# The first two jobs of the first output projection, placed ahead of the last two projection jobs of the first layer

## The chip, the cores and the metric

The kernel runs on one core of one Trainium2 chip. The metric is device time in microseconds, as the median of the runs of a kernel; lower is better. Engines are named as in the profile: PE (TensorE matmul), PEld (its weight loads), DVE (VectorE), ACT (ScalarE), POOL (GpSimd) and SP (SyncE, which issues the DMAs here).

## What is computed

Two layers on a sequence of 2048 frames with 1024 features, each `x = x + gate * Mixer(RMSNorm(x) * (1 + scale) + shift)`, and a final RMSNorm. The change lies at the end of the first layer, whose mixer is a gated linear recurrence:

```python
def rglru_block(h, in_w, conv_w, conv_b, gate_w, gate_b, lam, out_w):
    proj = h @ in_w
    xb, zg = proj[..., :D_RNN], proj[..., D_RNN:]
    xb = causal_dwconv(xb, conv_w) + conv_b
    pre = einsum('bsni,knij->kbsnj', xb.reshape(...), gate_w) + gate_b
    r_t, i_t = sigmoid(pre)
    log_a = -RG_C * r_t * softplus(-lam)
    a_t = exp(log_a)
    b_t = sqrt(-expm1(2.0 * log_a)) * (i_t * xb)
    _, hseq = lax.associative_scan(_lin_combine, (a_t, b_t), axis=1)
    return (hseq * silu(zg)) @ out_w
```

The second layer's mixer is a chunked gated delta rule with its own input and output projections; its first input weights are already being loaded while the first layer ends.

## The kernel before

**Tiles.** All matrix products are made of 128x512 results. Each factor is split into a high and a low part, and a product of depth 1024 takes 8 depth tiles of three matmuls each: high by high, low by high, high by low. One such product, 24 matmuls into one PSUM bank, is a **job** (`job` L663 for input projections, `out1_jobs` L933 for the first output projection; both call `products`, whose matmul is L668). PSUM has four bank pairs, called `mm`, `d`, `c` and `tp`.

**The end of the first layer.** The sequence is handled in two units of 1024 frames, each in two halves of 512. Of the second unit the last four input jobs are, in order: x panel 7 on half 0, z panel 7 on half 0, x panel 7 on half 1, z panel 7 on half 1 (named x70, z70, x71 and z71 below; in the trace the tiles `hh_('in1', 1)_1833` belong to half 0, `..._2277` to half 1). An x job's result goes through the convolution (ACT `xf` L746, `edge` L752, three DVE taps L756), is split into `xh` (ACT L798) and `xl` (DVE L801), and then PE makes two gate products `pg` of three matmuls each (L807). Behind these come ACT tanh `tg` (L857), `th`, `tg` (L817, L819), a square root (L830, with a table load ahead of it), DVE steps, a scan (L838), and POOL's product with `tz` (L845), which SP stores as `y_d` (L849). A z job's result goes through ACT tanh `tz` (L783) and DVE (L785).

**The first output projection.** Its 32 jobs take, for two blocks of 128 frames at a time, column half d=0 of both blocks and then column half d=1 of both. Its left factor `yh`, `yl` (ACT L925, DVE L929) comes from `y_d`. d=0 uses the bank pair `mm` and d=1 the pair `d`. A job's result waits for a tile `xr` of the input (SP L970), is multiplied with the gate and added to `xr` on DVE (L954, L956), and stored to `x1_d` (SP L959). The `xr` tiles share two places with `xl`, and their loads begin only when x71's `xl` has its place.

**Weights, and the two places they go through.** A weight panel is loaded by SP into `raw` (L606), cast on ACT to `whi` (L644), and POOL makes `wlo` from `raw` and `whi` (L650). There are two places for `raw`, two for `whi` and two for `wlo`. The output weights use the same two `raw` places: each column half is loaded in four parts `oraw` (SP L896), each split into `oh` (ACT L907) and `ol` (DVE L909). The weights of d=0 (`oh_2402`) are ready long before. Those of d=1 (`oh_3984`) take the room of z70's input, so their splits begin after z70. The `raw` places are taken, in this order, by: the second layer's first panel, d=1 part 0, the second layer's second panel, and d=1 parts 1, 2 and 3. The second layer's first `whi` takes the place of x panel 7, so its cast waits for x71's last matmul.

**The order of the work.** Every step is a generator, and `Weave` lays them out before the kernel runs: it picks the thread that can start first by a table of assumed durations, then by priority. The result is a fixed list of instructions for each engine and for SP, which each engine works through in order. `project_thread` (L698) is the thread that runs all projection jobs one after another.

Of the kernel before, what the change touches and what calls it, by code (L numbers as in the profile page):

```python
# [19 lines left out]
NU = S // T  # L20
# [119 lines left out]
def trunk_kernel(ctx, tc, x, c, ada_w, ada_b, ada_c, norm_c, final_g, w1, cw1, cb1, gate_w, gate_b, lam, ow1,  # L140
# [91 lines left out]
    def ev(*key):  # L232
        return events.setdefault(key, Event())

    def put(tag, token):
        w.put(slots[tag], token)
# [344 lines left out]
    def pair(a, b):  # L581
        return [(p, i) for i in range(NTC) for p in (a, b)]

    plans = []
    for u in range(NU):
        panels = [(1, kind, n) for n in range(KT) for kind in "xz"]
        jobs = pair(*panels[:2]) + [(p, i) for p in panels[2:-2] for i in range(NTC)] + pair(*panels[-2:])
        plans.append((("in1", u), panels, jobs))
    plans.append((("out1",), [], []))
    for u in range(NU):  # L590
# [4 lines left out]
        jobs = pair(*panels[:2]) + [(p, i) for p in panels[2:-2] for i in range(NTC)] + pair(*panels[-2:])  # L595
# [65 lines left out]
    def products(pt, lhs, rhs, wait=None, dur=MM):  # L661

        for k in range(KT):  # L663
            if wait is not None:
                yield wait(k)
            for n, (a, b) in enumerate(((0, 0), (0, 1), (1, 0))):
                yield "pe", dur, 0.0
                pe.matmul(pt, lhsT=lhs[a][:, k, :], rhs=rhs[b][:, k, :], start=(k == 0 and n == 0),  # L668
                          stop=(k == KT - 1 and n == 2))

    def job(name, jobs, n):
        u = name[1]
        p, i = jobs[n]
        layer, kind, m = p
        hi, lo, htok, ltok = yield ev("w", name, p)
        h = yield ev("tiles", (name, i))
        rtok = None
        if layer == 2 and kind in "kq":
            rtok = yield slots[kind + "t"]

        bank = ("d" if layer == 1 else "c") if kind in "vz" else "mm"
        mtok = yield slots[bank]
        pt = ps.tile([P, TC], F32, tag=bank, name="mm")
        yield from products(pt, (hi, lo), h, (lambda k: ev("split", (name, i), k)), 0.2275 if layer == 1 else MM)
        if all(q != p for q, _ in jobs[n + 1:]):
            put("whi", htok)
            put("wlo", ltok)
        if layer == 1:
            w.spawn((conv1_thread if kind == "x" else z1_thread)(u, m, i, pt, mtok, bank), 2, 0.2)
        elif kind == "z":  # L690
            w.spawn(zgate_thread(u, m, i, pt, mtok, bank), 6, 0.2)
        else:
            w.spawn(conv2_thread(u, kind, m, i, pt, mtok, bank, rtok), 5, 0.2)
        if all(j != i for _, j in jobs[n + 1:]):
            w.set(ev("free", name, i))
        w.set(ev("job", name, n))

    def project_thread():  # L698
        for name, panels, jobs in plans:
            if name == ("out1",):  # L700
                yield from out1_jobs()
                continue
            for n in range(len(jobs)):
                if name == ("in1", 0) and n < 2:

                    w.spawn(job(name, jobs, n), 8 + n)
                    if n == 1:
                        yield ev("job", name, 0)
                        yield ev("job", name, 1)
                else:  # L710
                    yield from job(name, jobs, n)
        yield from out2_jobs()
# [217 lines left out]
            put("yf", tok)  # L930
            w.set(ev("yhl", b), (yh, yl, htok, ltok))

    def out1_jobs():  # L933
        nb = S // P
        jobs = [(b + q, d) for b in range(0, nb, 2) for d in range(2) for q in range(2)]
        for b, d in jobs:
            yh, yl, htok, ltok = yield ev("yhl", b)
            ow = yield ev("owtiles", 1, d)
            bank = "d" if d else "mm"
            mtok = yield slots[bank]  # L940
            pt = ps.tile([P, TC], F32, tag=bank, name="mmo")
            yield from products(pt, (yh, yl), ow, (lambda k: ev("ow", 1, d, k // 2 * 2)))
            if d == 1:
                put("yh", htok)
                put("yl", ltok)
            w.spawn(residual1_thread(b, d, pt, bank, mtok), 3, 0.2)
            if b == nb - 1:
                w.set(ev("free", "out1", d))

    def residual1_thread(b, d, pt, bank, mtok):  # L950
        xr, xtok = yield ev("xr", b, d)
        row = yield ev("gate", 0, d)
        yield "dve", EV
        dve.tensor_tensor(pt, pt, row[:, d * TC:(d + 1) * TC], ALU.mult)  # L954
        yield "dve", EV
        dve.tensor_tensor(xr, pt, xr, ALU.add)  # L956
        put(bank, mtok)
        yield "sp", 256 * KB
        sp.dma_start(out=x1_d[b * P:(b + 1) * P, d * TC:(d + 1) * TC], in_=xr)  # L959
        put("xr", xtok)  # L960
        w.set(ev("x1", b, d))
# [632 lines left out]
    def out2_jobs():  # L1594
        nb = S // P

        parts = {b: [(0, TC), (TC, TC)] for b in range(nb - 1)} | {nb - 1: [(0, TC), (TC, TC // 2), (TC + TC // 2, TC // 2)]}
        jobs = [(0, 0), (1, 0), (0, 1), (1, 1)] + [(b, q) for b in range(2, nb) for q in range(len(parts[b]))]
        for b, q in jobs:
            c0, n = parts[b][q]  # L1600
            d, o = divmod(c0, TC)
            yh, yl, htok, ltok = yield ev("ohl", b)
            ow = yield ev("owtiles", 2, d)
            if q == 0:
                w.spawn(finish_thread(b, len(parts[b])), 3, 3.0)
            mtok = yield slots["mm"]
            pt = ps.tile([P, n], F32, tag="mm", name="mmo")
            yield from products(pt, (yh, yl), [t[:, :, o:o + n] for t in ow],
                                (lambda k: ev("ow", 2, d, k // 2 * 2)), MM * n / TC)
            if q == len(parts[b]) - 1:  # L1610
                put(*htok)
                put(*ltok)
            w.spawn(final_thread(b, q, c0, n, pt, mtok), 3, 0.2)
# [63 lines left out]
    with tc.manual_schedule():  # L1677
# [3 lines left out]
        in1, in2 = [("in1", u) for u in range(NU)], [("in2", u) for u in range(NU)]  # L1681
# [7 lines left out]
        w.spawn(columns_thread(), 4)  # L1689
        w.spawn(panels_thread(), 1)  # L1690
        w.spawn(project_thread(), 9)
        w.spawn(lru_thread(), 4)
        w.spawn(row_halves_thread([(0, 2, 0), (0, 2, 1), (1, 0, 0), (1, 0, 1), (1, 1, 0), (1, 1, 1), (1, 2, 0),
# [95 lines left out]
```

## Time and profile before

| | us |
|---|---|
| runs | 1933.47, 1934.21, 1941.75 |
| median | 1934.21 |
| span of the profiled execution, first to last instruction | 1937.1 |
| PE busy in it | 1844.0 |
| DVE, ACT and POOL busy in it | 1471.2, 1048.2, 654.8 |

The profiled execution has no other time of its own than its span, which lies 2.9 us above the median of the runs. In timeline rows the first number is the start in us, the second the duration in us; brackets give the engine's idle time ahead of the instruction and what ended it. Ends of matmuls are modelled, so neighbouring matmuls overlap in the rows, and the distance between starts is what one costs.

### The profile page before, as it was taken

Reading aid. Unit: us, or ns where it says so; the run is one execution under the profiler, and the core shown is the slowest. Engines: PE = TensorE matmul, PEld = TensorE weight load, DVE = VectorE, ACT = ScalarE, POOL = GpSimd, SP = SyncE. Lnnn points to the kernel's source line nnn. Section 1 sums busy time; section 2 is a strip of 40 time slices with the busy share of each in tenths; the row PEclk is TensorE's granted clock in tenths of the full one; section 3 lists DMA queues with packets and bytes.
Section 4 is the critical chain, followed back from the end, with each engine's and each line's share of the span. In section 5 each row is a group of like instructions: output and inputs, shape, how many; then the busy total and the mean of one; then the engine's idle time right before and its main releaser. Section 6 shows DMA issues by size and latency. Waiting matters only on the chain.

```text
span 1937.1 us, 31289 instructions
## 1 busy us (share of the span) xinstructions
PE 1844.0 (95%) x10286; PEld 1503.9 (78%) x10286; DVE 1471.2 (76%) x3175; ACT 1048.2 (54%) x2587; POOL 654.8 (34%) x1116
## 2 busy tenths in 40 slices
PE   6999999999899999898999999999999999999998
PEld 3787778878688877677787877788888888888887
DVE  6898998887544668869888896769777878886653
ACT  3666677667212345375565663565666656654321
POOL 3344542223100235345445543333332334411110
PEclk9999999999899999999999998999999999999999
DMA  8476746554578735446676565555365555687751
GB/s 320 116 219 189 223 138 220 175 167 138 169 204 236 208 106 145 128 111 160 166 186 141 138 158 150 149 156 158 102 163 143 140 140 139 155 246 207 230 161 66
DMA packets 511723, 322.77 MB, mean 167 GB/s; under 512 B 371268, under 2 KB 439236, under 8 KB 511560
## 3 DMA queue, kind: packets, MB, share of 16 engines
q1 hardware_dynamic: 511560, 320.77, 59.1%
q8 instruction: 81, 1.33, 0.3%
q14 instruction: 82, 0.67, 0.1%
HBM read 219.93 MB, written 100.73 MB: 166 GB/s over the span
## 4 chain that ended last, share of the span: by engine, by line
PE 61%; DVE 20%; DMA 6%; issue 4%; ACT 4%; SPq 3%; POOL 2%; DVEq 0%; POOLq 0%; ACTq 0%
PE mm L668 31%; PE mmo L668 16%; DVE xf L718 2%; DVE ttmp L1292 2%; DVE tblk L1295 2%; PE pg L807 1%; PE py L1429 1%; PE pp L1412 1%; PE pS L1442 1%; PE pqk L1257 1%; PE pS L1441 1%; PE pp L1413 1%; PE pkk L1169 1%; DVE xf L756 1%; DMA raw<-in_w 1%
## 5 line engine op out<-in xcount | busy, mean ns | idle before, releaser
L718 DVE SCALAR_TENSOR_TENSOR xf<-xe,cw_s,xf 128x512 f32<-128x512 f32 x288 | 224.9, 784 | 20.6 <-POOL xf L997 18.1
L650 POOL TENSOR_TENSOR wlo<-raw,whi 128x1024 fp32r<-128x1024 f32 x48 | 120.9, 2519 | 143.6 <-ACT whi L644 115.4
L1292 DVE TENSOR_TENSOR ttmp<-blk,tblk 128x60 f32<-128x60 f32 (+24 forms) x496 | 125.4, 253 | 16.6 <-DMA blk<-blk_d 5.4
L1295 DVE TENSOR_TENSOR tblk<-tblk,ttmp 128x60 f32<-128x60 f32 (+24 forms) x496 | 124.8, 252 | 10.7
L644 ACT CAST whi<-raw 128x1024 fp32r<-128x1024 f32 x96 | 100.2, 1044 | 50.3 <-DMA raw<-in_w 44.5
L668 PE MATMUL mmo<-oh,yh 128*128 128x512 f32 x256 | 102.1, 399 | 4.8 <-ACT oh L907 4.8
L668 PE MATMUL mm<-hh_('in2', 0)_5342,whi 128*128 128x512 f32 x256 | 105.3, 411 | 0.0
L668 PE MATMUL mm<-hh_('in2', 0)_5437,whi 128*128 128x512 f32 x256 | 105.3, 411 | 0.0
L668 PE MATMUL mmo<-ol,yh 128*128 128x512 f32 x256 | 102.2, 399 | 3.0 <-DVE ol L909 3.0
L668 PE MATMUL mm<-hh_('in2', 0)_5342,wlo 128*128 128x512 f32 x256 | 104.7, 409 | 0.0
L668 PE MATMUL mm<-hl_('in2', 0)_5343,whi 128*128 128x512 f32 x256 | 104.7, 409 | 0.0
L668 PE MATMUL mm<-hl_('in2', 0)_5438,whi 128*128 128x512 f32 x256 | 104.1, 407 | 0.0
L668 PE MATMUL mm<-hh_('in2', 1)_12030,wlo 128*128 128x512 f32 x256 | 104.1, 407 | 0.0
L668 PE MATMUL mm<-hl_('in2', 1)_12219,whi 128*128 128x512 f32 x256 | 104.0, 406 | 0.0
L668 PE MATMUL mm<-hh_('in2', 0)_5437,wlo 128*128 128x512 f32 x256 | 103.9, 406 | 0.0
L668 PE MATMUL mm<-hh_('in2', 1)_12218,whi 128*128 128x512 f32 x256 | 103.6, 405 | 0.0
L668 PE MATMUL mm<-hh_('in2', 1)_12030,whi 128*128 128x512 f32 x256 | 103.5, 404 | 0.0
L668 PE MATMUL mm<-hl_('in2', 1)_12031,whi 128*128 128x512 f32 x256 | 103.3, 403 | 0.0
L668 PE MATMUL mm<-hh_('in2', 1)_12218,wlo 128*128 128x512 f32 x256 | 103.2, 403 | 0.0
L668 PE MATMUL mmo<-ol,oh 128*128 128x512 f32 (+1 forms) x264 | 103.1, 391 | 0.0
L668 PE MATMUL mmo<-oh,ol 128*128 128x512 f32 (+1 forms) x264 | 103.1, 391 | 0.0
L668 PE MATMUL mmo<-oh,oh 128*128 128x512 f32 (+1 forms) x264 | 103.0, 390 | 0.0
(331 smaller groups left out, 5649.8 us busy)
## 6 DMA issues: line engine op xcount, KB each, us to landing
raw<-in_w SPq DMA_DIRECT2D x96, 512.0 KB, 4.2
araw<-in_ada_w SPq DMA_DIRECT2D x32, 512.0 KB, 4.3
xt<-x_d SPq DMA_DIRECT2D x32, 512.0 KB, 4.9
xt_d<-xb SPq DMA_DIRECT2D x192, 64.0 KB, 2.4
xk<-xt_d SPq DMA_DIRECT2D x24, 512.0 KB, 6.1
xt<-in_x SPq DMA_DIRECT2D x16, 512.0 KB, 4.4
ada<-in_ada_w SPq DMA_DIRECT2D x16, 512.0 KB, 8.5
y_d<-tz SPq DMA_DIRECT2D x32, 256.0 KB, 3.2
```

Of the source, the lines that this page charges most:

```text
L644: act.copy(hi, raw)
L650: pool.tensor_tensor(lo, raw, f(hi), ALU.subtract)
L668: pe.matmul(pt, lhsT=lhs[a][:, k, :], rhs=rhs[b][:, k, :], start=(k == 0 and n == 0), stop=(k == KT - 1 and n == 2))
L718: dve.scalar_tensor_tensor(xf, xe[:, 1 + j:1 + j + TC], wc[:, j:j + 1], xf, ALU.mult, ALU.add)
L756: dve.scalar_tensor_tensor(xf[:, 3:TC], pt[:, j:j + TC - 3], wc[:, j:j + 1], xf[:, 3:TC], ALU.mult, ALU.add)
L807: pe.matmul(pg, lhsT=a[:, g, :], rhs=b, start=(q == 0), stop=(q == 2))
L1169: pe.matmul(pkk[:, b, :], lhsT=kc, rhs=kc, start=True, stop=True)
L1257: pe.matmul(pqk[:, b, :], lhsT=kt[:, b * P:(b + 1) * P], rhs=qt[:, b * P:(b + 1) * P], start=True, stop=True)
L1292: dve.tensor_tensor(tmp, blk[:, j, j + 1:32].unsqueeze(2).to_broadcast([P, r, c_]), t[:, j, 0:c_].unsqueeze(1).to_broadcast([P, r, c_]), A ...
L1295: dve.tensor_tensor(t[:, j + 1:32, 0:c_], t[:, j + 1:32, 0:c_], tmp, ALU.subtract)
L1412: pe.matmul(pp[:, 0, :], lhsT=kc, rhs=S_, start=True, stop=True)
L1413: pe.matmul(pp[:, 1, :], lhsT=qc, rhs=S_, start=True, stop=True)
```

## The change

The first two of the 32 output jobs (d=0 of blocks 0 and 1) run between z70 and x71 instead of behind z71, and write to the bank pair `tp` instead of `mm`. The other 30 jobs and all other code stay.

```diff
@@ project_thread
             if name == ("out1",):
-                yield from out1_jobs()
+                yield from out1_jobs(False)
                 continue
             for n in range(len(jobs)):
+                if name == ("in1", NU - 1) and n == len(jobs) - 2:
+                    yield from out1_jobs(True)
                 if name == ("in1", 0) and n < 2:
@@
-    def out1_jobs():
+    def out1_jobs(first):
         nb = S // P
         jobs = [(b + q, d) for b in range(0, nb, 2) for d in range(2) for q in range(2)]
-        for b, d in jobs:
+        for b, d in jobs[:2] if first else jobs[2:]:
             yh, yl, htok, ltok = yield ev("yhl", b)
             ow = yield ev("owtiles", 1, d)
-            bank = "d" if d else "mm"
+            bank = "tp" if first else "d" if d else "mm"
             mtok = yield slots[bank]
```

Two lines come in, so the lines behind L700 have numbers higher by two in the changed kernel. `Weave` lays the order out again. On PE the 48 matmuls of the two jobs move ahead of the 48 of x71 and z71, and the two gate products of x71 stand right behind z71 instead of in the second moved job; on every engine the order is the same again a few tens of instructions later.

The list of ACT before, at the end of the first layer. `raw8_3982` is the second layer's first panel, `mm_4067` the result of x71, `mm_4002` that of z70.

```order
L798 CAST xh_4116<-xf1_4054 128x512 [waits DVE_49]
L644 CAST whi_4123<-raw8_3982 128x1024 [waits DMAHW0_49,PE_49]
L857 ACTIVATE tg_4143<-pg_4135,gb_s_96 128x512 [waits PE_49]
L746 ACTIVATE xf1_4150<-mm_4067,cb1_s_95,cw1_s_94 128x509 [waits DVE_49]
L752 COPY edge1_123<-mm_4067 128x3
L830 ACT_TABLE_LOAD
L830 ACTIVATE tg_4038<-tg_4038 128x512
```

The list of ACT now, at the same place; x71 is `mm_4156`, z71 `mm_4196`, d=1 part 0 `oraw_4237`, the second layer's second panel `raw16_4239`.

```order
L748 ACTIVATE xf1_4198<-mm_4156,cb1_s_95,cw1_s_94 128x509 [waits DVE_49,PE_49]
L754 COPY edge1_123<-mm_4156 128x3
L644 CAST whi_4208<-raw8_3982 128x1024 [waits DMAHW0_49]
L832 ACT_TABLE_LOAD
L832 ACTIVATE tg_4140<-tg_4140 128x512 [waits DVE_49]
L785 ACT_TABLE_LOAD [waits DMAHW6_49,PE_49]
L785 ACTIVATE tz_4248<-mm_4196 128x512 [waits Pool_49]
L800 CAST xh_4251<-xf1_4198 128x512 [waits DVE_49]
L909 ACTIVATE oh_1_3984<-oraw_4237 128x1024 [waits DMAHW7_49]
L644 CAST whi_4256<-raw16_4239 128x1024 [waits DMAHW0_49]
```

The cast of the second layer's first panel stood ahead of x71's convolution and stands behind it now; x71's `xh` and the first split of the d=1 weights stand behind z71's `tz`.

The list of SP before, from the last stores of the gate row on. `oraw_4161`, `oraw_4249`, `oraw_4254` are parts 0, 1 and 2 of the d=1 weights.

```order
L849 DMA y_d_69<-tz_3977 128x512 [waits DMAHW5_49,Pool_49]
L896 DMA oraw_4161<-in_ow1 128x1024 [waits DMAHW7_49,DMAHW6_49]
L606 DMA raw16_4163<-in_w2 128x1024 [waits DMAHW0_49,Pool_49]
L658 DMA wlo_d2k0_4140<-wlo_4109 128x1024
L970 DMA xr_4188<-in_x 128x512 [waits DMAHW1_49]
L970 DMA xr_4242<-in_x 128x512 [waits DMAHW2_49,DVE_49,PE_49]
L896 DMA oraw_4249<-in_ow1 128x1024 [waits DMAHW6_49,DMAHW3_49,DVE_49]
L896 DMA oraw_4254<-in_ow1 128x1024 [waits DMAHW7_49,DMAHW4_49,Pool_49]
```

The list of SP now; parts 0, 1 and 2 are `oraw_4237`, `oraw_4284` and `oraw_4290`.

```order
L851 DMA y_d_69<-tz_3977 128x512 [waits DMAHW5_49,Pool_49]
L851 DMA y_d_69<-tz_4052 128x512 [waits DMAHW6_49,Pool_49]
L898 DMA oraw_4237<-in_ow1 128x1024 [waits DMAHW7_49]
L606 DMA raw16_4239<-in_w2 128x1024 [waits DMAHW0_49,Pool_49]
L972 DMA xr_4243<-in_x 128x512 [waits DMAHW1_49]
L658 DMA wlo_d2k0_4218<-wlo_4195 128x1024 [waits DMAHW2_49]
L972 DMA xr_4277<-in_x 128x512 [waits DMAHW3_49,DVE_49,PE_49]
L898 DMA oraw_4284<-in_ow1 128x1024 [waits DMAHW4_49,DMAHW0_49,Pool_49]
L898 DMA oraw_4290<-in_ow1 128x1024 [waits DMAHW7_49,DMAHW5_49,DVE_49]
```

A store of `y_d` has moved ahead of part 0. Part 1 waited for DVE (part 0's `ol`) and part 2 for POOL (the second panel's `wlo`); now part 1 waits for POOL and part 2 for DVE. Part 3 waits, before and now, for DVE's `ol` of part 1.

## The prediction

> **What bounds the kernel now.** I read the page first, then the busy times by stretch around the end of the first layer, the timeline of PE there, and the chain of waits of the same stretch. On the page the share of PE's busy time says what the whole is made of:
>
> ```profile
> PE 1844.0 (95%) x10286; PEld 1503.9 (78%) x10286; DVE 1471.2 (76%) x3175; ACT 1048.2 (54%) x2587; POOL 654.8 (34%) x1116
> ```
>
> Some 93 us of the span have no matmul in them, so a change of order can only win back a place where PE stands still, or make one. Busy times by stretch, with the granted clock behind the bracket of POOL, show one such place, between the end of d=0 of blocks 0 and 1 and the middle of their d=1:
>
> ```profile
> 490.20:508.00 17.80, 10.08 (x25) 7.16 (x26) 12.54 (x14) 8.01 (x9) 4.82 (x5) 0.71 0.54 179
> 508.00:520.00 12.00, 12.00 (x53) 9.75 (x52) 4.34 (x6) 1.05 (x1) 0.00 (x0) 1.00 0.55 176
> ```
>
> In the first stretch PE is busy for 10.08 of 17.80 us at a granted clock of 0.71; in the next it is full. The timeline of PE says what it waits for:
>
> ```profile
> 489.77 0.39 PE L668 MATMUL mmo<-oh,yl 128*128 128x512 f32 x1
> 493.75 0.53 PE L668 MATMUL mmo<-oh,yh 128*128 128x512 f32 x1 [3.59 <-ACT oh L907]
> 496.50 0.79 PE L668 MATMUL mmo<-ol,yh 128*128 128x512 f32 x1 [2.22 <-DVE ol L909]
> ...
> 503.77 0.50 PE L668 MATMUL mmo<-ol,yh 128*128 128x512 f32 x1 [0.76 <-DVE ol L909]
> 504.11 0.44 PE L668 MATMUL mmo<-oh,yl 128*128 128x512 f32 x1
> 504.35 0.63 PE L668 MATMUL mmo<-oh,yh 128*128 128x512 f32 x1
> ...
> 507.76 0.39 PE L668 MATMUL mmo<-oh,yl 128*128 128x512 f32 x1
> ```
>
> PE waits for the split weights of d=1: for parts 1 and 2 at 493.75 and 496.50, for part 3 at 503.77. From the start at 489.77 to the one at 507.76 there are 24 steps of a matmul (the stretch's 25 rows hold one more behind 507.76). At the pace of a full PE, 0.233 us a step (worked out below), they would take 5.6 us; they take 17.99. So this place costs 12.4 us, and that is the most that any new order around it can win.
>
> Why the weights are late is in the chain of waits of this stretch (start, duration, what):
>
> ```profile
> 475.34 5.53 DMA raw<-in_w
> ...
> 482.08 2.41 POOL wlo L650
> ...
> 486.22 5.91 DMA y_d<-tz
> ...
> 495.31 1.15 DVE ol L909
> 496.45 0.02 issue
> 496.47 4.91 DMA oraw<-in_ow
> ...
> 501.40 1.07 ACT oh L907
> ...
> 502.49 1.24 DVE ol L909
> 503.73 0.04 issue
> 503.77 11.27 PE mmo L668 x41
> ```
>
> The two `raw` places pass between the second layer's first panels and the parts of d=1. Part 3 can be loaded only when part 1 is split (495.31), and is used at 503.77. Between the second panel's `wlo` and that split lies a detour: the store of `y_d` at 486.22, which held up z71's `tz`, and with it the splits queued behind it on ACT and DVE.
>
> **The change, part by part.** The matmuls are the same ones, so PE's work as such costs nothing either way. What counts is when x71 and z71 end, since ACT's list hangs on both. PE's rows at the start of x71 and at the start of the two output jobs:
>
> ```profile
> 463.69 0.40 PE L668 MATMUL mm<-hh_('in1', 1)_2277,whi 128*128 128x512 f32 x1
> ...
> 476.03 0.40 PE L668 MATMUL mmo<-oh,yh 128*128 128x512 f32 x1
> ```
>
> 48 matmuls of x71 and z71 and six of the gates lie between them: 12.34 us, 0.2285 each. From 476.03 to 489.77 are 59 steps of output matmuls and gates: 13.74 us, 0.233 each. x71 ended before at 463.69 + 24 x 0.2285 = 469.17. Now the two output jobs stand there, with the gates of x70 among them: 54 x 0.233 = 12.58 us, to 476.27. x71 then ends at 481.75 and z71 at 487.23. Up to here PE has no reason to stop: the d=0 weights and `yh`, `yl` of both blocks are ready (no wait on them stood ahead of 476.03), and `tp` has no other user here but the last sums of the conditioning, done by then.
>
> Everything that hangs on x71 is 12.6 us later. First of all the second layer's first `whi`, whose place x71 gives free, on ACT's list:
>
> ```profile
> 469.15 1.06 ACT L644 CAST whi<-raw 128x1024 fp32r<-128x1024 f32 x1
> 472.80 0.69 ACT L857 ACTIVATE tg<-pg,gb_s 128x512 f32<-128x512 f32 x1 [2.59 <-PE pg L807]
> 473.39 0.77 ACT L746 ACTIVATE xf<-mm,cb_s,cw_s 128x509 f32<-128x509 f32 x1
> 474.05 0.16 ACT L752 COPY edge<-mm 128x3 f32<-128x3 f32 x1
> 474.23 1.28 ACT L830 ACT_TABLE_LOAD   x1
> 475.52 0.63 ACT L830 ACTIVATE tg<-tg 128x512 f32<-128x512 f32 x1
> 476.17 1.28 ACT L783 ACT_TABLE_LOAD   x1
> 477.47 0.60 ACT L783 ACTIVATE tz<-mm 128x512 f32<-128x512 f32 x1
> 477.96 0.62 ACT L798 CAST xh<-xf 128x512 fp32r<-128x512 f32 x1
> ```
>
> The cast ran at 469.15, the moment x71 ended. Now the chain is this, each duration from the rows above. x71's last result is there at 481.9 (the start of its last matmul plus the 0.39 of a row). `xf` and `edge` come first: 0.66 + 0.18, start to start, so the cast begins at 482.75 and ends at 483.8. POOL's `wlo`, 2.41, ends at 486.3, and its `raw` place is free. The second panel's load, 5.53, lands at 491.8; its cast, 1.06, ends at 492.95; its `wlo`, 2.41, at 495.4. The list of SP says that part 1 waits for POOL, so its load goes then and lands, 4.91 later, at 500.35. `oh`, 1.07, and `ol`, 1.24, end at 502.7; part 3's load lands at 507.65; its `oh` and `ol` end at 510.0, and PE takes it at 510.05. Before it was 503.77: **6.3 us later**. Of the 12.6 us the chain gives back half: the store of `y_d` now goes ahead of the `oraw` loads, POOL takes the first `wlo` at once (before, it began 2.7 us behind its cast: 2.41 ahead of the load at 475.34 against the cast's end at 470.2), and nothing but the splits stands on ACT when part 1 lands.
>
> Two other queues run beside this chain and must not be later than it. ACT's next table load waits for z71, at 487.4; then 1.30 (table, start to start), 0.49 (`tz`), 0.62 (`xh`) and 1.07 (`oh` of part 0) end at 490.9, ahead of the panel's landing at 491.8. That is 0.9 us of cover. SP's second `xr`, queued ahead of part 1, waits for x71's gates, which wait for `xl` behind z71's `tz` on DVE:
>
> ```profile
> 478.10 0.69 DVE L785 SCALAR_TENSOR_TENSOR tz<-tz,mm 128x512 f32<-128x512 f32 x1 [0.41 <-ACT tz L783]
> 478.70 1.28 DVE L838 TENSOR_TENSOR_SCAN tg<-th,hcar,tg 128x512 f32<-128x512 f32 x1
> 479.90 0.67 DVE L801 TENSOR_TENSOR xl<-xf,xh 128x512 fp32r<-128x512 f32 x1
> ```
>
> ACT's `tz` ends at 489.3; DVE's three steps take 0.60 + 1.20 + 0.67, so `xl` is there at 491.8. The five gate matmuls behind it take 1.2 us, or at half the clock twice that: done at 493.0 to 494.4, ahead of 495.4 by 1.0 or more. If that cover goes, every us beyond is one on the path.
>
> PE itself now stops twice: from 487.2 to about 490 and 492 for the gates, and from about 495 to 500 and on for parts 1 to 3. The first of these is new, and lies wholly beside the chain. Behind part 3's arrival the lists agree again, and I take the slow matmuls there to be the same: at 504.35 one starts every 0.43 us, and at 507.76 the pace is back, eight steps at 0.2 us too much, 1.6 us, in both kernels. Bounds: the three loads on the path could take 4.91 each (0.6 us less) or as long as the 5.91 of the store (2.4 us more); I take the like for the like, 5.53 for the panel amid stores and 4.91 for the parts. Should part 1 after all get the place of part 0, whose `ol` ends near 493.5, all is 1.9 us earlier. The slow matmuls can be nil (1.6 less) or twice as many (1.6 more). Together +2 to +10 around 6.3.
>
> The Trainium skill, "TensorE: Matmul & The Clock Gate", Part 1, says that PE's clock is halved after an idle window of about 3.4 us and given back after a busy one, and that the window runs freely, so that the same kernel shows different numbers of slow matmuls. By it the tail behind part 3 would be up to 3.4 us at half rate, an estimate of 0 to 1.7 us, in either kernel, and the sum would move by no more than 1.7 us to either side. The rows from 503.77 to 507.76, 4.0 us, are near it.
>
> All later work hangs on the output jobs: the second layer's input is made from `x1_d`, so I let the 6.3 us through whole. The profiled span would be 1937.1 + 6.3 = 1943.4; the median of the runs lies 2.9 below that span, so the forecast for it is 1934.2 + 6.3 = **1940.5 us**.
>
> **The rivals.** *The stall goes.* If the move gave the four parts time to arrive, PE would run through: 1934.2 - 12.4 = 1921.8. For it speaks that ACT and DVE have less to do while the moved jobs run, and that the idle place is just behind them. Against it: d=1 would be wanted at about 488, and the `raw` place for part 1 passes through two casts, of which the first cannot begin before 481.9. 4 in 100.
>
> *It washes out.* The 6.3 us are swallowed, since the loads are quicker and a later place that waits for something else has slack, or since part 1 gets part 0's place and the slow matmuls vanish (1.9 + 1.6 + 0.6 = 4.1 of the 6.3): 1934 to 1936. 12 in 100.
>
> *The gates take over the path.* SP's `xr` is queued ahead of parts 1 and 2. If PE's clock is halved and `xh` is held by ACT, x71's gates can end later than 495.4; from there each us counts, for both parts, and also for `tg`, `th`, `tg` on ACT (0.69 + two of about 0.8), which stand ahead of the split of part 1. Gates done at 499 instead of 494.4 make it 6.3 + 3.6 = 9.9: 1944.1 or more, slower by over 0.5%. For it speaks the cover of only 1 us; against it that every term is from a row. 13 in 100.
>
> **How the numbers follow.** The forecast, +2 to +9.7, has 71 in 100. 0.5% is 9.7 us, about what a measurement of this kernel can tell from no change. Faster by more than that is the first rival alone, 0.04; slower by more, the third, 0.13; within it the forecast and the second, 0.83. The range leaves out the first rival, what of the second lies under 1934.5, and the far end of the third: 1934.5 to 1945.5, which is +0.3 to +11.3.
>
> **What would show it.** In the changed kernel's timeline: x71 ending near 481.7 and z71 near 487.2 without a stall before; the first panel's `whi` near 482.7; the second panel's load issued near 486.3; parts 1 and 2 issued near 495.4 and part 3 near 502.7; PE's last wait for `ol` ending near 510. Wrong would be parts 1 and 2 issued ahead of 490, or part 3 used before 504, or a `raw` place that waits for something not named here; and a stage behind it whose own shift is not that of part 3.

## The result

| | median, us | runs | ratio to the kernel before | 95% interval |
|---|---|---|---|---|
| before | 1934.66 (1931.08 to 1941.75) | 9 | | |
| changed | 1945.73 (1941.76 to 1956.22) | 9 | 1.0052 | 1.0039 to 1.0065 |
| changed, once more | 1942.19 (1936.52 to 1950.43) | 12 | 1.0032 | 1.0014 to 1.0050 |

The changed kernel is slower, by 10.1 us as the first ratio has it and by 6.2 as the second. The forecast was 6.3 more, at 1940.5 us, in a range of 1934.5 to 1945.5. The first median lies 0.2 us above that range; taken as a difference from the kernel before, 11.1 us by the medians and 10.1 by the ratio, it lies inside the +0.3 to +11.3, near the upper end. The intervals of the two comparisons overlap. The second comparison and all later runs were timed beside runs of the kernel before on the same chip, whose medians were 1935.3, 1936.45 and 1935.35 us.

### The profile page after: what moved, and what is told of

The parts are those of the page before. It is cut to its first block, busy times and chain, and to the rows that moved or that the text cites. A ratio compares the mean times of both kernels' runs of the same rounds, so it can differ in the third digit from the quotient of the medians.

```text
span 1944.6 us, 31285 instructions
## 1 busy us (share of the span) xinstructions
PE 1850.2 (95%) x10286; PEld 1508.3 (78%) x10286; DVE 1474.5 (76%) x3175; ACT 1044.8 (54%) x2587; POOL 648.8 (33%) x1116
## 4 chain that ended last, share of the span: by engine, by line
PE 56%; DVE 20%; DMA 12%; ACT 4%; issue 4%; SPq 3%; POOL 2%; DVEq 0%; POOLq 0%; ACTq 0%
PE mm L668 29%; PE mmo L668 14%; DVE xf L720 3%; DVE tblk L1297 2%; DVE ttmp L1294 2%; DMA x_d<-xr 1%; PE py L1431 1%; DMA araw<-in_ada_w 1%; DVE acc L410 1%; PE pp L1414 1%; DMA xt<-x_d 1%; DVE xf L758 1%; PE pS L1444 1%; PE pqk L1259 1%; PE pg L809 1%
## 5 line engine op out<-in xcount | busy, mean ns | idle before, releaser
L668 PE MATMUL mmo<-oh,yl 128*128 128x512 f32 x256 | 102.8, 401 | 0.4 <-DVE yl L931 0.4
```

## The profile after

The page of the changed kernel: the span is 1944.6 us against 1937.1, with PE busy for 1850.2 against 1844.0.

```profile
span 1944.6 us, 31285 instructions
PE 1850.2 (95%) x10286; PEld 1508.3 (78%) x10286; DVE 1474.5 (76%) x3175; ACT 1044.8 (54%) x2587; POOL 648.8 (33%) x1116
```

Busy times by stretch (the number behind the bracket of POOL is the granted clock). The first stretch runs from the first moved matmul to the end of z71, the second over the waits, the third over the matmuls behind them.

```profile
466.82:490.00 23.18, 23.18 (x102) 18.99 (x101) 17.83 (x22) 15.61 (x20) 8.73 (x8) 1.00 0.18 46
490.00:512.50 22.50, 13.00 (x27) 7.43 (x25) 16.81 (x21) 12.25 (x14) 7.13 (x6) 0.62 0.77 254
512.50:524.00 11.50, 11.45 (x43) 9.24 (x44) 5.05 (x6) 2.09 (x2) 0.00 (x0) 0.85 0.35 118
```

PE runs through the two moved jobs, x71 and z71 without a stop, and then has one place with 13.00 of 22.50 us busy at a clock of 0.62; before, it was 10.08 of 17.80. The place is longer, not different in kind. PE's rows there (start, duration; in brackets the wait and what ended it):

```profile
466.82 0.39 PE L668 MATMUL mmo<-oh,yh 128*128 128x512 f32 x1
...
492.94 0.79 PE L809 MATMUL pg<-xh,gh 128*128 128x512 f32 x1 [2.52 <-ACT xh L800]
494.94 0.80 PE L809 MATMUL pg<-xl,gh 128*128 128x512 f32 x1 [1.21 <-DVE xl L803]
...
503.11 0.80 PE L668 MATMUL mmo<-oh,yh 128*128 128x512 f32 x1 [2.23 <-ACT oh L909]
504.37 0.80 PE L668 MATMUL mmo<-ol,yh 128*128 128x512 f32 x1 [0.47 <-DVE ol L911]
...
511.29 0.50 PE L668 MATMUL mmo<-oh,yh 128*128 128x512 f32 x1 [1.86 <-ACT oh L909]
512.55 0.51 PE L668 MATMUL mmo<-ol,yh 128*128 128x512 f32 x1 [0.76 <-DVE ol L911]
...
516.54 0.40 PE L668 MATMUL mmo<-oh,yl 128*128 128x512 f32 x1
```

The place begins at 466.82, before at 463.69. These 3.13 us have nothing to do with the change: the same work was 2.0 us late at 425 already, and a gate of x61 waited once for DVE, 0.85 us, which no other profile here shows. All times of this trace are therefore compared less 3.13. Part 3 is used at 512.55, 45.73 behind the start of the place; before it was 503.77, or 40.08. That is 5.65 us later. The full pace is back 3.99 us behind that, before 3.99 (503.77 to 507.76).

ACT's rows for the two casts of the second layer's panels, with x71's convolution:

```profile
485.02 0.78 ACT L748 ACTIVATE xf<-mm,cb_s,cw_s 128x509 f32<-128x509 f32 x1 [1.71 <-PE mm L668]
...
485.74 1.06 ACT L644 CAST whi<-raw 128x1024 fp32r<-128x1024 f32 x1
...
493.74 1.03 ACT L644 CAST whi<-raw 128x1024 fp32r<-128x1024 f32 x1
```

And SP's rows (here the duration is SP's own, not the transfer's): the second panel at 489.30, the second `xr` at 497.04, parts 1 and 2 from 497.48, the third `xr` at 505.24, part 3 at 505.67.

```profile
489.30 0.33 SPq L606 DMA_DIRECT2D raw<-in_w  x1
...
497.04 0.33 SPq L972 DMA_DIRECT2D xr<-in_x  x1
497.48 1.20 SPq L898 DMA_DIRECT2D oraw<-in_ow  x2
...
505.24 0.33 SPq L972 DMA_DIRECT2D xr<-in_x  x1
505.67 0.37 SPq L898 DMA_DIRECT2D oraw<-in_ow  x1
```

The chain of waits that ended last in this stretch has a link that the prediction did not have:

```profile
490.49 1.28 ACT L785
...
491.78 0.60 ACT tz L785
...
493.02 1.28 DVE tg L840
494.30 0.32 DVE xl L803
...
494.80 0.69 DVE mmo L956
495.49 2.84 DVE ol L911
498.33 0.61 DVE xr L958
...
498.96 6.21 DMA x_d<-xr
...
505.24 0.33 SPq L972
...
505.67 4.49 DMA oraw<-in_ow
...
511.27 1.24 DVE ol L911
```

Part 3's load stands in SP's list behind the third `xr`. That `xr` takes the place of the first moved job's result, so it waits until the result is stored to `x1_d` (498.96, 6.21 us). The store waited for the sum on DVE, which stood behind part 0's `ol`, and that, with the scan, `xl` and the product ahead of it, behind z71's `tz`. The `raw` place for part 3 was free when part 1's `ol` was made, at 504.32 (DVE's row below: 503.09 and 1.23); the load went at 505.67. So two chains of nearly the same length end here, and the new one was later by 1.3 us. In the kernel before, the third and the fourth `xr` stood ahead of part 3 too, but the later of them went 0.95 us before part 3's load (496.47), so the link cost nothing there:

```profile
495.52 0.33 SPq L970 DMA_DIRECT2D xr<-in_x  x1
```

In the second profile of the changed kernel it is the same link again:

```profile
498.12 6.47 DMA x_d<-xr
...
505.09 5.56 DMA oraw<-in_ow
...
513.03 1.22 PE mmo L668 x2
```

## The experiments

Single runs of one kernel differ by several microseconds at places that have nothing to do with this one. So each experiment is read in two ways: by its ratio, and by the **delay of the place**. The delay is how much later one and the same matmul behind the place starts (the fourth high-by-high one of the seventh output job), counted from the start of the place, than in the profile of before. That matmul's rows, in before, in the changed kernel, and in the kernel before with late panels (below):

```profile
525.34 0.39 PE L668 MATMUL mmo<-oh,yh 128*128 128x512 f32 x1
```

```profile
534.11 0.39 PE L668 MATMUL mmo<-oh,yh 128*128 128x512 f32 x1
```

```profile
513.15 0.39 PE L668 MATMUL mmo<-oh,yh 128*128 128x512 f32 x1
```

For the changed kernel it is (534.11 - 466.82) - (525.34 - 463.69) = 67.29 - 61.65 = +5.6 us. All kernels in one table:

| kernel | place begins | that matmul | delay, us | ratio | 95% interval |
|---|---|---|---|---|---|
| before | 463.69 | 525.34 | | | |
| before, again | 465.25 | 527.29 | +0.4 | 1.0003 | 0.9987 to 1.0019 |
| bank alone | 465.25 | 527.12 | +0.2 | 0.9995 | 0.9983 to 1.0006 |
| one job moved | 466.98 | 532.43 | +3.8 | 1.0022 | 1.0004 to 1.0039 |
| changed | 466.82 | 534.11 | +5.6 | 1.0052 | 1.0039 to 1.0065 |
| changed, again | 465.98 | 535.41 | +7.8 | 1.0032 | 1.0014 to 1.0050 |
| changed, part 3 first | 463.34 | 531.45 | +6.5 | 1.0029 | 1.0013 to 1.0046 |
| between x71 and z71 | 466.76 | 530.02 | +1.6 | 1.0004 | 0.9990 to 1.0019 |
| before, late panels | 463.91 | 513.15 | -12.4 | 0.9941 | 0.9919 to 0.9963 |
| changed, late panels | 465.57 | 518.58 | -8.6 | 0.9956 | 0.9940 to 0.9972 |
| between, late panels | 466.48 | 515.93 | -12.2 | 0.9972 | 0.9954 to 0.9991 |

**Both kernels again.** No edit.

> The kernel before, once more, to see how much a time and a trace differ without any edit. Place of interest: from the first matmul that follows z70 to PE's use of part 3 of the d=1 weights (the low part). Chain theory (the change costs what the chain through the two raw places loses, and nothing elsewhere): 40.1 us there, as in the first trace (463.69 to 503.77), ratio 1.000 within its interval. Rival theory (the change costs some 5 us more at places outside the chain): the same for this kernel; if this kernel alone differs from the kernel before by 0.2% or more, the measured 0.5% can't be split at that grain.

> The changed kernel, once more. Chain theory: the place takes 45.6 us as in the first trace (466.98 to 512.55), 5.5 more than before, and the ratio is 1.003 (1.002 to 1.004), the 1.005 measured first being partly chance. Rival theory: the place takes 5.5 us more, but the ratio is 1.005 again, and the missing 5 us show at another place of the trace or as a place that varies from run to run.

The kernel before comes out at 1.0003 and +0.4 us. The changed one has 1.0032, the first theory's ratio, and +7.8 us, 7.4 more than the second profile of before. Part 3 was used at 47.05 us, 1.4 later than was expected. Of the 7.4 us, 6.6 stand at part 3 (513.03 - 465.98 = 47.05, against 505.73 - 465.25 = 40.48) and 0.8 in the slow matmuls behind it. So the place costs 5.6 to 7.4 us.

**The bank alone.** The two jobs stay behind z71 and use the bank pair of the transposes.

```diff
-                yield from out1_jobs()
+                yield from out1_jobs(True)
+                yield from out1_jobs(False)
...
-            bank = "d" if d else "mm"
+            bank = "tp" if first else "d" if d else "mm"
```

> The first two output jobs stay behind z71 and only take the bank pair tp instead of mm. Chain theory: x71 and all loads are where they were, so the place takes 40.1 us (39.5 to 41) and the ratio is 1.000. Rival theory (the other bank pair costs, here or in a later stage that uses tp): the place is the same, the ratio 1.002 to 1.003.

It came out at 0.9995 and +0.2 us: the bank costs nothing that these runs can tell.

**One job moved.** In the changed kernel, only the first job goes ahead of x71.

```diff
-        for b, d in jobs[:2] if first else jobs[2:]:
+        for b, d in jobs[:1] if first else jobs[1:]:
```

> Only the first output job (block 0, d=0) moves ahead of x71, in the bank pair tp; the second stays behind z71 in mm. x71 is 5.6 to 6.9 us later instead of 12.6. Chain theory: the chain through the raw places has 6.3 us of slack, so the place takes 41 us (40 to 42.5), 1 more than before, and the ratio is 1.0005 (0.9995 to 1.0015). Rival theory (each moved job costs alike): half of the change, 43 us at the place and 1.0025 in all.

It came out at 1.0022 and +3.8 us, between none and two, with part 3 used at 42.7 us (509.66 - 466.98). These are the numbers of the second theory; the 6.3 us of slack that the first one counted on are not there. The last link is that of the changed kernel: `ol` of part 1 was made at 500.73 (499.50 and 1.23 on DVE), and part 3 went at 501.70, behind the `xr` load. Of the 2.6 us at part 3, 1.0 stands at the end of part 1's split (33.75 us behind the start of the place, before 32.76), 1.0 behind the `xr`, and 0.6 in the transfer (5.56 us, before 4.91). The other 1.2 are slow matmuls behind part 3.

```profile
494.36 6.36 DMA x_d<-xr
...
500.79 0.33 SPq L972
...
501.70 5.56 DMA oraw<-in_ow
```

**Part 3 ahead of the `xr` loads.** The changed kernel, with SP's list mended so that the third `xr` load comes behind part 3.

```diff
         for b, d in [(b + q, d) for b in range(0, nb, 2) for d in range(2) for q in range(2)]:
+            if (b, d) == (0, 1):
+                yield ev("owissue", 1, 1)
             xtok = yield slots["xr"]
```

> The changed kernel, with the load of d=1 part 3 placed ahead of the third and later xr loads in SP's list; nothing else moves. In the changed kernel part 3's load was issued at 505.67, behind an xr load that waited for a store of x1_d, 1.3 us after its raw place was free (504.32). If the raw places are the cause and SP's order only adds to it, part 3 is issued when part 1 is split and used 1.3 us earlier, at about 44.4 us behind the start of the place: ratio 1.002 to 1.004. If SP's order is the main cause, part 3 is used near 40 to 41 us as before, ratio 1.000.

The load now goes the moment that part 1 is split, 37.2 us behind the start of the place (500.51 - 463.34), where it was 38.85 in the changed kernel (505.67 - 466.82). Yet part 3 is used at 45.7, as there and at neither of the expected times, and the ratio is 1.0029. The chain of waits shows where the gain went:

```profile
500.51 5.29 DMA oraw<-in_ow
...
506.91 2.12 DVE ol L911
```

The load took 5.29 us instead of 4.49, and `ol` 2.12 instead of 1.24. So SP's order is not the main cause. With the earlier issue the transfer and the split were longer by 1.7 us together, which is all that the issue had won (38.85 less 37.2). For the split the rows give a reason: POOL's `tz` of x71's gate row ended at much the same time in both, 44.3 us (511.10) and 44.6 us (507.94) behind the start of the place, and here `ol` starts while it runs (see the last section). Why the transfer was longer was not tried.

The same trace has one of the prediction's rivals on the path. SP's second `xr`, which waits for x71's gates, went last ahead of part 1:

```profile
491.45 2.09 PE pg L809 x4
...
493.56 0.33 SPq L974
...
493.99 4.15 DMA oraw<-in_ow
```

The second panel's `wlo` ended at 493.77, 0.2 us before that load.

**Between x71 and z71.** The jobs are moved past z71 alone, so that x71 ends as before.

```diff
-                if name == ("in1", NU - 1) and n == len(jobs) - 2:
+                if name == ("in1", NU - 1) and n == len(jobs) - 1:
                     yield from out1_jobs(True)
```

> The two output jobs moved only past z71: they stand between x71 and z71, in the bank pair of the transposes. x71 then ends as before, and with it the cast of the second layer's first panel. If the change costs by x71's delay, part 3 of d=1 is used 40 to 42 us behind the start of the place (before 40.1 and 40.5, changed 45.7 and 47.1), ratio 0.999 to 1.001. If it costs by the jobs standing ahead of z71 and its gate row, whichever job is moved past, it is 45 us or more, ratio 1.003 or more.

Ratio 1.0004 and +1.6 us. Part 3 was used at 43.3 (510.06 - 466.76), between the two expectations: x71's delay is most of the cost, but not all. What is left is, by the rows, ACT's list. In before the second panel's cast ran when its load had landed (475.34 and 5.53), far ahead of z71's `tz`:

```profile
480.95 1.06 ACT L644 CAST whi<-raw 128x1024 fp32r<-128x1024 f32 x1 [0.83 <-DMA raw<-in_w]
...
492.15 0.60 ACT L783 ACTIVATE tz<-mm 128x512 f32<-128x512 f32 x1 [0.43 <-DMA y_d<-tz]
```

Here the load went as early (478.41, 11.65 us behind the start of the place in both), but the cast stands behind that `tz`, 9.2 us later:

```profile
492.72 0.60 ACT L785 ACTIVATE tz<-mm 128x512 f32<-128x512 f32 x1
493.21 1.04 ACT L644 CAST whi<-raw 128x1024 fp32r<-128x1024 f32 x1
```

**Late panels.** The other way to test the two `raw` places: the second layer's first panels stand behind all four parts of d=1. The parts then have both places for themselves, and PE's work is the same. The wait for `gates` in the next line moves with the edit. One edit, made in the kernel before, in the changed one and in the one between:

```diff
-                if m == 2 and name == ("in2", 0):
+                if m == 0 and name == ("in2", 0):
                     yield ev("owt", 1, 1)
                     yield ev("gates")
```

> The kernel before, with the second layer's first panels loaded only when all four parts of the d=1 weights have been loaded, so that these parts have the two raw places for themselves; the same work in all. If the raw places and what they wait for set the time of part 3, the four parts are split by about 489 us, where d=1 begins: PE's idle 12.4 us at that place go, the time is about 1922 to 1926, ratio 0.993 to 0.996. The other theory: PE stands still there for reasons that stay (the bank's turn, ACT's and DVE's lists, or the panels being late for the next stage): at most a third of it goes, ratio 0.998 or more.

The stall is gone. Busy times of this kernel from the start of the place to the matmul of the table:

```profile
463.91:490.00 26.09, 26.09 (x115) 21.33 (x114) 23.85 (x34) 21.34 (x28) 8.60 (x8) 1.00 0.34 112
490.00:513.15 23.15, 23.15 (x101) 18.63 (x100) 16.08 (x18) 5.54 (x7) 8.88 (x7) 1.00 0.80 247
```

PE is busy throughout, at full clock, and the place is 12.4 us shorter, as much as the prediction had put down as its loss. The median was 1922.41 us, ratio 0.9941: 11.4 us of 1936.45 (the medians lie 14.0 apart). It is faster than both kernels. The edit does not separate two things: with the panels, their casts on ACT, their products on POOL and their loads leave this stretch as well. It shows that the panels ahead of the parts make the stall, not how much of it goes through the places alone.

> The changed kernel, with the same later loading of the second layer's first panels. If the change costs only what the weights of d=1 lose by it, it costs nothing once they are early: the same time as the kernel before with late panels, within 2 us, ratio 0.993 to 0.996 to the kernel before. The other theory: the two jobs cost something of their own where they stand now (the bank pair, the gates behind z71, the conditioning): 5 us or more above the kernel before with late panels, ratio 0.997 or more.

With late panels the changed kernel is at 0.9956 and -8.6 us: the weights cost it nothing any more, but the place is still 3.8 us longer than in the kernel before with late panels. The ratio lies in the first expectation's range, but the two times are 2.9 us apart by the ratios and some 6 by the medians, so neither the 2 us of the first nor the 5 of the second is settled by them; by the place neither holds. One wait of PE is left:

```profile
509.79 0.79 PE L668 MATMUL mmo<-oh,yl 128*128 128x512 f32 x1 [2.16 <-DVE yl L931]
```

It is for the second factor of block 3. On DVE this `yl` stands behind the scan of x71's gate row, which is late with x71. Ahead of that scan DVE also stood still once for 1.7 us, up to a sum at 505.94, and the profile names no reason. Slow matmuls behind the wait make up the rest.

> Late panels, and the two output jobs between x71 and z71 in the bank pair of the transposes, so that x71 is not delayed. With late panels the changed order left one wait of PE, 2.16 us for the second factor yl of block 3, which stood on DVE behind x71's gate row; the order before left none. If that wait comes from x71's delay, it is gone here and PE runs through from z70 to blocks 2 and 3: as the kernel before with late panels, ratio 0.992 to 0.996, no wait of PE over 0.5 us in the place. If moving the jobs past z71 alone does it, a wait of 2 us or more for yl is there again.

Without x71's delay that wait is gone; PE waits for nothing in the place, and the delay is -12.2, as with the order before. The ratio of 0.9972 is higher than was expected. The trace has a loss behind the place: from there to 680 PE waits 4.3 us for `yh` and `yl`, where the order before with late panels waits 1.6 over the same length of time. Why these come late there was not tried. Its waits (what PE waited for: us in total, times, the longest):

```profile
PE mmo L668 <- DVE yl L931: 3.0, 5, 0.9
PE mmo L668 <- ACT yh L927: 1.3, 3, 0.8
```

## Why the prediction was right, and where it was not

**What bounds the place: right, and to its size.** It put the 12.4 us down to the passing of the two `raw` places between the panels and the parts, and late panels gave 12.4 back; the share of the places alone is not shown. Two of its readings are off, and enter no sum: the waits at 493.75 and 496.50 are both for part 1 (`oh`, then `ol`), not for parts 1 and 2, and 495.31 is the start of part 1's split, which ended at 496.45.

**The moved jobs run through: right.** PE was busy for 23.18 of 23.18 us.

**The chain through the `raw` places: right up to part 1.** Less 3.13 us, x71's convolution began at 481.89 (forecast 481.9), the first cast at 482.61 (482.75), the second panel's load at 486.17 (486.3), the loads of parts 1 and 2 at 494.35 (495.4). The last is 1.05 early since the panel took 4.4 us from its issue to its cast (489.30 to 493.74) instead of 5.53. The cover for SP's second `xr` was used up, where the forecast had 1.0 us: it went at 497.04, `wlo` ended at 497.24, and SP had part 1's load out only at 497.48.

**The step that failed: part 3 does not wait for `ol` of part 1 alone.** The prediction, and the section on the change ahead of it, put part 3's load right behind that split. It looked at SP's second `xr`, ahead of part 1, and not at the third, ahead of part 3. Behind that one stands a chain of its own, from z71 over DVE and the store of `x1_d`. It held part 3 until 505.67, or 502.54 less the shift. That is close to the 502.7 of the forecast only because two errors cancel: `ol` of part 1 was made 1.5 us earlier than forecast (504.32 less 3.13 is 501.19), and 1.35 us were lost behind the `xr`. So the forecast for part 3 (+6.3, measured +5.7 and +6.6) was right in size with one link wrong; that it came so close is luck. Mending that link alone gave nothing back. A term in the new link is part 0's `ol`, 2.93 us where the forecast had 1.24. Had it taken 1.24, the sum, the store and the third `xr` would by these rows have been 1.7 us earlier (an estimate), and that `xr` out of the way before 504.32.

**"The slow matmuls are the same": half right.** They took 3.99 us in the first pair of profiles, in both kernels. In the second pair they took 0.8 us more in the changed kernel. Over all orders with the stall, the time from part 3's use to the matmul of the table went from 1.6 us less than before (between x71 and z71) to 1.2 more (one job moved), inside the bounds that the prediction gave.

**"I let it through whole": not shown for a single run.** In the first pair of profiles the later work keeps the shift: 8.8 us behind the place (534.11 - 525.34), 7.5 at the end (the spans). In the second pair 8.1 us behind the place (535.41 - 527.29) have become -0.8 at the end (spans of 1940.5 and 1941.3), with waits of later stages that differ from run to run. Only the medians can tell: 6.2 us of the second comparison are the forecast, 10.1 of the first (7.5 to 12.6 by its interval) are over it. The place accounts for 5.6 to 7.4 of these; whether the other 2.7 to 4.5 us of the first comparison are chance, and where they would lie, stays open.

**The rivals.** The stall did not go, and the cost was not washed out. The gates did not take over the path to part 3, though they used up their cover and held part 1 by 0.2 us; the neighbour of that rival, a third `xr` held by DVE, did.

## What to carry to other kernels

Where a load waits for a place, read what stands ahead of it in the issuing queue for every one of the loads, not only the first: an entry that waits for a store of another stage holds them all. And ask which user of a shared place can wait: moving matmuls about the stall cost 6 us or more, while letting the panels that nobody needed yet wait gave 11.

## What the runs showed of the hardware

A DVE split beside a POOL product waits for the whole of it. In the changed kernel, DVE's `ol` of part 0 and of part 1:

```profile
495.40 2.93 DVE L911 SCALAR_TENSOR_TENSOR ol<-oraw,oh 128x1024 fp32r<-128x1024 f32 x1
503.09 1.23 DVE L911 SCALAR_TENSOR_TENSOR ol<-oraw,oh 128x1024 fp32r<-128x1024 f32 x1 [0.84 <-ACT oh L909]
```

and POOL's `wlo` beside the first:

```profile
494.88 2.36 POOL L650 TENSOR_TENSOR wlo<-raw,whi 128x1024 fp32r<-128x1024 f32 x1
```

`wlo` ends at 497.24 and `ol` at 498.33, 1.09 behind it, about as long as `ol` takes alone (1.23). With part 3 first it was the same: POOL's row `tz` ends at 507.94 and DVE's `ol` at 509.02, 1.08 behind it.

```profile
506.67 1.27 POOL L847 TENSOR_TENSOR tz<-tz,tg 128x512 f32<-128x512 f32 x1
```

The Trainium skill, "SBUF — State Buffer", section "SBUF: two separate sides", says that a port pair is shared by the two engines as an exclusive lock: whoever starts first has it for the whole instruction, and a DVE operation with two SBUF inputs waits for a GpSimd one that reads SBUF. These rows agree. In the forecast `ol` had 1.24 us throughout; part 0's 1.7 us more are a part of the chain that held part 3.

The stores of `x1_d` that stand in the chains took 6.2 to 6.5 us amid the loads of weights.
